# Half-size products for the down projection of two groups of SwiGLU tiles, with one gate/up unit placed in front of them

## The chip, the cores and the metric

The kernel runs on one core of a Trainium2 chip. The metric is the device time of one execution in microseconds. The time before is the median of three runs, 1265.05 us (1262.17 to 1267.66).

The core has five engines with a queue of instructions each, worked in order: TensorE (PE; its weight loads are listed as PEld), VectorE (DVE), ScalarE (ACT), GpSimd (POOL) and SyncE (SP). SP and POOL issue the transfers from memory here. An engine waits for another one by a semaphore, and everything behind the waiting instruction in its queue waits too.

## The reference

Two layers of an encoder on 512 tokens of width 1024. Each layer has a block of two attention-like halves (retention and differential attention) and a SwiGLU block. The change touches the SwiGLU block alone:

```python
h = rms_norm(x, ffn_norm_g[l])
x = x + (jax.nn.silu(h @ w_gate[l]) * (h @ w_up[l])) @ w_down[l]
```

`D_FF` is 2816, which is 22 tiles of 128. Everything is float32.

## The kernel before

**Layout.** Activations lie transposed: a tile has 128 features on the partitions and the 512 tokens along the row. `x` is eight such tiles, and the SwiGLU activation is 22. Products keep float32 accuracy by a split into two parts: `hi` is a rounded copy made by ACT (a CAST), `lo = src - hi` is made by DVE, and a product is three matmuls, hi·hi, hi·lo and lo·hi. So each weight and each activation that enters a product costs a cast on ACT and a subtraction on DVE of its size. The weights are the stationary side, so each matmul has a weight load of its own.

**The groups.** The SwiGLU block runs over the tiles in four groups, `FFN = [(0, 4), (4, 12), (12, 18), (18, FT)]` (L34). For each group, gate and up are computed tile by tile, and then the down projection of that group is added to the eight tiles of `x` (the loop over `m`; L205 to L207 are its matmuls, three for each tile of the group, 512 columns each; L634 is the addition to `x`).

**The plain group.** Group (0, 4) uses `gate_up`, with whole products of 512 columns. Beside it, DVE and ACT prepare with `combine` (L714 to L738) the sums of quarter blocks of h that the later groups need.

**The units.** For all later tiles, `seven` (from L754) computes gate and up of one tile, as a 2x2 block product, by seven half-size products in place of eight (the scheme of Strassen and Winograd): each product is 4 x 3 matmuls of 256 columns (L775), so 84 matmuls for a unit. The weight has four blocks of 512 columns. Three of the seven left sides are blocks as they are, and four are sums: `s31` holds two sums, made by transfers (a broadcast copy by SP, L756, and on top of it an accumulating transfer by POOL, L759); `a` gets its second half from DVE (the sum at L760); `s4` comes from DVE (L763). Then `split_in` splits three buffers of 1024 columns (ACT L740, DVE L741) and `split` splits `s4` (L223, L224). The products' sums go from three PSUM banks through ACT (L780, L783, L786) and DVE (L787, L789, L793, L795, L796), with a Silu on ACT (L106), and the result is split (L223, L224) for the down products.

**What sets the order.** A scheduler fixes the order of each engine's queue at build time, from data dependencies, free buffers and its own durations. By hand, units are interleaved: a unit's splits and first product stand ahead of the last product of the unit before. There are three buffers for the `hi` and three for the `lo` of weights (`NHL`), so a unit's three splits reuse those of the unit before as its products finish; weights land in three `raw` and three `ah` buffers (`four`), which is two units' worth. From the second unit on, the sum at L760 is kept behind the last split of the unit before (`last_split`, "unit by unit"); the first unit of each layer has no such tie.

Of the kernel before, what the change touches and what calls it, by code (L numbers as in the profile page):

```python
# [9 lines left out]
F32R = mybir.dt.float32r  # L10
AF = mybir.ActivationFunctionType
ALU = mybir.AluOpType

P = 128
# [19 lines left out]
FFN = [(0, 4), (4, 12), (12, 18), (18, FT)]  # L34
# [20 lines left out]
def encoder_kernel(ctx: ExitStack, tc: tile.TileContext, xT, wfirst, wsingle, wvv, wout, wgu, wdn, prm, lam, cst, outT):  # L55
# [15 lines left out]
    def big(s, dt=F32, tag="w", bufs=NW):  # L71
        return tpool.tile([P, T], dt, tag=tag, name=nm(s), bufs=bufs)
# [19 lines left out]
    def f32(ap):  # L92
        return ap.bitcast(F32)
# [84 lines left out]
    def parts():  # L178
        return tuple(wpool.tile([P, 1024], F32R, tag=t, name=nm(t), bufs=NHL) for t in ("hi", "lo"))
# [30 lines left out]
    def cut(pair, *idx):  # L210
        return tuple(t[idx] for t in pair)
# [9 lines left out]
    def split(src, tag, bufs):  # L221
        hi, lo = pair() if tag == "h" else [big(n, F32R, tag, bufs) for n in ("hi", "lo")]
        nc.scalar.copy(hi, src)  # L223
        nc.vector.tensor_tensor(lo, src, f32(hi), op=ALU.subtract)  # L224
        return hi, lo

# [83 lines left out]
    def layer(l, n1, h, x_src, first_raw):  # L310
# [395 lines left out]
        comb = []  # L706
# [8 lines left out]
        def combine(i):  # L715
# [14 lines left out]
            tb = split(tb, *(("mix", NMIX) if i else ("qk", NQK)))  # L730
            comb.append(
# [6 lines left out]
        def split_in(raw):  # L738
            hi, lo = parts()
            nc.scalar.copy(hi, raw)  # L740
            last_split[0] = nc.vector.tensor_tensor(lo, raw, f32(hi), op=ALU.subtract).ins.name  # L741
            return [(hi[:, i * T : (i + 1) * T], lo[:, i * T : (i + 1) * T]) for i in range(2)]
# [6 lines left out]
        fours, last_split = [0], [None]  # L749

        def seven(ff, act, tag, bufs):

            src = wgu[l, ff].rearrange("p (i n) -> p i n", n=T)
            s31, a, b, s4 = four(), four(), four(), big("s4")  # L754
            sums = s31.rearrange("p (i n) -> p i n", n=T)
            nc.sync.dma_start(sums, src[:, 1:2].broadcast_to([P, 2, T]))  # L756
            nc.sync.dma_start(a[:, :T], src[:, 0])
            nc.sync.dma_start(b, wgu[l, ff][:, 1024:])
            nc.gpsimd.dma_start(sums, src[:, 0::3], accum_op=ALU.add)  # L759
            i = nc.vector.tensor_tensor(a[:, T:], a[:, :T], s31[:, T:], op=ALU.add)  # L760
            if last_split[0]:
                tc.add_manual_dep(i.ins, last_split[0], order, reason="unit by unit")
            nc.vector.tensor_tensor(s4, b[:, :T], a[:, T:], op=ALU.add)  # L763
            g1, s2 = split_in(a)
            s3, s1 = split_in(s31)
            g2, u2 = split_in(b)
            s4 = split(s4, *(("w", NW) if ff >= FFN[-1][0] else ("mix", NMIX)))

            pa, pb, pc = (bank() for bank in (acc_bank, sc_bank, out_bank))

            def product(ps, w, r, start):
                for k in range(4):
                    L, R = cut(w, slice(None), slice(k * P, (k + 1) * P)), comb[k][r]
                    for i, (x1, x2) in enumerate(((0, 0), (0, 1), (1, 0))):
                        nc.tensor.matmul(ps[:, :C], L[x1], R[x2], start=start and k + i == 0, stop=k == 3 and i == 2, skip_group_check=True)  # L775
# [18 lines left out]
            func(g, g, AF.Silu)  # L794
            nc.vector.scalar_tensor_tensor(u[:, H1], pa[:, :C], -1.0, g[:, H1], op0=ALU.mult, op1=ALU.mult)  # L795
            nc.vector.tensor_tensor(u[:, H2], u[:, H2], g[:, H2], op=ALU.mult)  # L796
            act.append(split(u, tag, bufs))

        for a0, a1 in FFN:
            act, last = [], a1 == FT  # L800
            if a1 <= PLAIN:
                for ff in range(a0, a1):
                    act.append(gate_up(ff, *(("mix", NMIX) if ff < 2 else ("rn", 4))))
                    if ff:
                        combine(ff - 1)
            else:
                units = []
                for ff in range(a0, a1):
                    tag = ("h", 8) if not last else ("mix", NMIX) if ff < a0 + 2 else ("rn", 4)
                    units.append(seven(ff, act, *tag))  # L810
                next(units[0])
                for i, unit in enumerate(units):
                    next(unit)
                    if i + 1 < len(units):
                        next(units[i + 1])
                    next(unit, None)
            n = (a1 - a0) * P
            for m in range(KT):

                both = 2 * n <= 1024  # L820
                if not both or m % 2 == 0:
                    new = new_chunk(n * (1 + both), 1)
                    for i in range(1 + both):
                        nc.sync.dma_start(new[0][:, i * n : (i + 1) * n], wdn[l, m + i][:, a0 * P : a1 * P])
                    ww = split_chunk(*new)
                w = cut(ww, slice(None), slice(m % 2 * n, (m % 2 + 1) * n)) if both else ww
                if last and l + 1 == DEPTH and m == KT - 1:

                    for t, queue in ((H1, nc.sync), (H2, nc.scalar)):
                        ps = any_bank()  # L830
                        for i, a in enumerate(act):
                            mm3(ps[:, :C], cut(w, slice(None), slice(i * P, (i + 1) * P)), cut(a, slice(None), t), i == 0, i == a1 - a0 - 1)
                        nc.vector.tensor_tensor(x[m][:, t], x[m][:, t], ps[:, :C], op=ALU.add)
                        queue.dma_start(outT[m][:, t], x[m][:, t])
                    continue
                ps = any_bank()
                for i, a in enumerate(act):
                    mm3(ps, cut(w, slice(None), slice(i * P, (i + 1) * P)), a, i == 0, i == a1 - a0 - 1)
                if last and l + 1 < DEPTH:
                    residual(m, x[m], ps, n3, h3, PRM_AG + 8 * (l + 1))  # L840
                    nc.sync.dma_start(xscr[m], x[m])
                else:
                    residual(m, x[m], ps, None, None, None)
                    if a1 <= PLAIN and m == 1:
                        combine(PLAIN - 1)
                    if last:
                        nc.sync.dma_start(outT[m], x[m])
# [30 lines left out]
def _layout(inputs):  # L878
# [30 lines left out]
    a["wdn"] = w.transpose(0, 3, 2, 1, 4).reshape(DEPTH, KT, P, FT * P)  # L909
# [41 lines left out]
```

## Time and profile before

| | |
|---|---|
| median of three runs | 1265.05 us |
| the profiled execution's own time | 1264.07 us |
| its span, first to last instruction | 1262.3 us |
| its mean granted TensorE clock | 0.999 |
| matmul records | 7516 |
| first read of the plain group's gate and up sums (L690), layer by layer | 302.0 us and 926.6 us |
| last addition of a down projection to `x` (L634), last layer | 1256.6 us |

The profile is one execution. An engine's busy time is a union over the span; a busy PE need not be a PE at its peak, since matmuls overlap. In a timeline row, the number in brackets is the time the engine stood idle before the row, and what ended it. `raw`, `s` (the `ah` buffers), `hi`, `lo` are weights; `b`, `bh`, `bl`, `ta`, `tb` are the sums of h; `acc`, `sc`, `o` are PSUM banks. The names of a row in a queue's order carry a number, so that equal names can be told apart.

### The profile page before, as it was taken

The page shows a single profiled execution, that of the slowest core. Times are in us where ns is not written, and L with a number is a line of the kernel's source. Part 1 is how long each engine was busy: PE and PEld are TensorE (multiplying, and loading weights), DVE is VectorE, ACT ScalarE, POOL GpSimd, SP SyncE. Part 2 cuts the span into 40 slices and gives each one's busy share as a digit, 9 for nine tenths or more (in the row PEclk, how much of TensorE's full clock was granted, in tenths as well). Part 3 has the DMA queues.
Part 4 walks back from the last instruction along what each step waited for, and adds up shares of the span by engine and source line. Part 5 has one row for each costly group of instructions (what it writes and reads, how often), then busy time and mean ns, then how long its engine had stood idle before and what let it go on. Part 6 is the DMA issues. An engine that isn't in the chain of part 4 may idle for free.

```text
span 1262.3 us, 19138 instructions
## 1 busy us (share of the span) xinstructions
PE 1247.4 (99%) x7516; PEld 1100.3 (87%) x7516; DVE 915.8 (73%) x1514; ACT 674.1 (53%) x1106; POOL 61.4 (5%) x78
## 2 busy tenths in 40 slices
PE   9999999999899999999999999999999999999998
PEld 7878988778799989989888889987887999899897
DVE  6899768867877546747568997697778775576574
ACT  6778746555445425525448785565553553254251
POOL 1000000000011001000000000000000110000000
PEclk9999999999999999999999999999999999999999
DMA  7222223243277537646342122142333774476452
GB/s 264 84 68 67 68 67 125 68 116 101 71 176 174 166 102 166 163 114 151 110 156 84 51 84 67 51 150 77 99 101 84 174 182 129 119 180 152 122 140 84
DMA packets 58842, 148.48 MB, mean 118 GB/s; under 512 B 5632, under 2 KB 5888, under 8 KB 58624
## 3 DMA queue, kind: packets, MB, share of 16 engines
q1 hardware_dynamic: 48528, 127.95, 32.8%
q0 software_dynamic: 9792, 18.88, 9.4%
q8 instruction: 59, 0.97, 0.3%
q10 hardware_dynamic: 432, 0.44, 0.1%
q14 instruction: 31, 0.25, 0.1%
HBM read 143.05 MB, written 4.19 MB: 117 GB/s over the span
## 4 chain that ended last, share of the span: by engine, by line
PE 94%; DVE 3%; DMA 1%; ACT 1%; issue 0%; ACTq 0%
PE acc L775 16%; PE acc L205 11%; PE acc L207 11%; PE acc L206 11%; PE o L775 8%; PE o L205 4%; PE o L207 4%; PE sc L775 4%; PE o L206 4%; PE sc L207 4%; PE sc L205 4%; PE sc L206 3%; PE sc L400 2%; PE o L501 2%; PE sc L485 1%; DMA raw<-in_wgu 1%
## 5 line engine op out<-in xcount | busy, mean ns | idle before, releaser
L194 ACT CAST hi<-raw 128x1024 fp32r<-128x1024 f32 (+2 forms) x139 | 138.2, 1002 | 185.8 <-issue 49.2
L198 DVE TENSOR_TENSOR lo<-raw,hi 128x1024 fp32r<-128x1024 f32 (+2 forms) x140 | 162.1, 1162 | 58.8 <-ACT hi L194 58.4
L205 PE MATMUL acc<-h,hi 128*128 128x512 f32 x406 | 160.1, 396 | 0.6 <-ACT hi L194 0.6
L206 PE MATMUL acc<-h,hi 128*128 128x512 f32 x406 | 159.4, 393 | 0.0
L207 PE MATMUL acc<-h,lo 128*128 128x512 f32 x406 | 159.4, 393 | 0.0
L775 PE MATMUL acc<-hi,hi 128*128 128x256 f32 x432 | 123.2, 285 | 0.0
L775 PE MATMUL acc<-hi,lo 128*128 128x256 f32 x432 | 122.3, 283 | 0.0
L775 PE MATMUL acc<-lo,hi 128*128 128x256 f32 x432 | 122.3, 283 | 0.0
L740 ACT CAST hi<-raw 128x1024 fp32r<-128x1024 f32 x54 | 56.7, 1050 | 72.3 <-PE acc L775 42.2
L741 DVE TENSOR_TENSOR lo<-raw,hi 128x1024 fp32r<-128x1024 f32 x54 | 66.2, 1225 | 38.1 <-ACT hi L740 38.1
L740 ACT CAST hi<-s 128x1024 fp32r<-128x1024 f32 x54 | 56.6, 1048 | 67.3 <-issue 25.6
L205 PEld LDWEIGHTS acc<-h,hi 128*128 128x128 f32 x406 | 76.5, 189 | 17.6 <-ACT hi L194 1.9
L207 PEld LDWEIGHTS acc<-h,lo 128*128 128x128 f32 x406 | 76.6, 189 | 16.1 <-DVE lo L198 0.2
L206 PEld LDWEIGHTS acc<-h,hi 128*128 128x128 f32 x406 | 76.6, 189 | 15.2
L741 DVE TENSOR_TENSOR lo<-s,hi 128x1024 fp32r<-128x1024 f32 x54 | 66.2, 1226 | 25.4 <-ACT hi L740 25.4
L775 PEld LDWEIGHTS acc<-lo,hi 128*128 128x128 f32 x432 | 82.9, 192 | 0.2
L775 PEld LDWEIGHTS acc<-hi,hi 128*128 128x128 f32 x432 | 82.7, 192 | 0.2
L775 PEld LDWEIGHTS acc<-hi,lo 128*128 128x128 f32 x432 | 82.8, 192 | 0.0
L106 ACT ACTIVATE g<-g 128x512 f32<-128x512 f32 x44 | 27.8, 632 | 52.7 <-DVE g L793 47.8
L106 ACT ACTIVATE sc<-sc,mx 128x512 f32<-128x512 f32 x64 | 46.0, 720 | 18.4 <-DVE mx L404 17.9
L205 PE MATMUL sc<-h,hi 128*128 128x512 f32 x142 | 55.5, 394 | 0.0
L206 PE MATMUL sc<-h,hi 128*128 128x512 f32 x142 | 55.4, 390 | 0.0
(235 smaller groups left out, 3500.4 us busy)
## 6 DMA issues: line engine op xcount, KB each, us to landing
raw<-in_wgu SPq DMA_DIRECT2D x52, 512.0 KB, 4.2
s<-in_wgu SPq DMA_DIRECT2D x36, 512.0 KB, 4.7
raw<-in_wsingle SPq DMA_DIRECT2D x32, 512.0 KB, 3.6
s<-in_wgu POOLq DMA_DIRECT2D x18, 512.0 KB, 6.4
raw<-in_wgu POOLq DMA_DIRECT2D x18, 512.0 KB, 7.3
raw<-in_wvv SPq DMA_DIRECT2D x16, 512.0 KB, 3.6
raw<-in_wout SPq DMA_DIRECT2D x16, 512.0 KB, 3.6
raw<-in_wdn SPq DMA_DIRECT2D x32, 256.0 KB, 2.9
```

Of the source, the lines that this page charges most:

```text
L106: i = nc.scalar.activation(out, src, f, **kw).ins
L194: c = nc.scalar.copy(hi[:, s], raw[:, s])
L198: nc.vector.tensor_tensor(lo[:, s], raw[:, s], f32(hi[:, s]), op=ALU.subtract)
L205: first = nc.tensor.matmul(out, L[0], R[0], start=start, stop=False)
L206: nc.tensor.matmul(out, L[0], R[1], start=False, stop=False)
L207: nc.tensor.matmul(out, L[1], R[0], start=False, stop=stop)
L400: nc.tensor.matmul(ps, q[m][:, t], k[m][part], start=part == 0, stop=part == 1)
L485: nc.tensor.matmul(out, ks[hh][part][:, sb], qs[hh][:, tb], start=part == 0, stop=part == 1)
L501: i = nc.tensor.matmul(o[b, c * C : (c + 1) * C], v[pr // 2][2 * c + j][:, (pr % 2) * P + hh * HD : (pr % 2) * P + (hh + 1) * HD], s[c][:, ...
L740: nc.scalar.copy(hi, raw)
L741: last_split[0] = nc.vector.tensor_tensor(lo, raw, f32(hi), op=ALU.subtract).ins.name
L775: nc.tensor.matmul(ps[:, :C], L[x1], R[x2], start=start and k + i == 0, stop=k == 3 and i == 2, skip_group_check=True)
```

## The change

The groups become (0, 4), (4, 10), (10, 16), (16, 22). The down projection of the two middle groups, six tiles each, is computed by seven half-size products as well: the six activation tiles are the two row halves (three pairs of tiles), the two token halves are the columns, and `x` tiles m and m + 4 are the two output halves. `seven` is generalised: it takes its weight, a block width `n` (512 for gate/up, 384 for down), the right sides and a function `finish`. A down unit is 7 products of 3 x 3 matmuls of 256 columns, 63 in all, and there are four for each group; its weights come from a new array `wds`, laid out on the host in blocks of 384 columns.

Since the right sides are now sums of pairs of activation tiles, the first three units of a group end with `first_parts` (b11 and t1), the last three with `second_parts` (b2, t2, t3 and t4). `down(m)` adds a unit's result to `x[m]` and `x[m + 4]`. The list of units of a layer is one sequence: six gate/up units, then one gate/up unit of the next group, four down units, and the other five gate/up units, and the same again. The down projection of groups (0, 4) and (16, 22) stays plain. The first unit's sum is tied behind the last split of `combine`. In the last plain down projection of layer 0, the parts of h for the next layer (`next_part`) of tiles 4 to 7 stand behind all eight additions.

```diff
-FFN = [(0, 4), (4, 12), (12, 18), (18, FT)]
+FFN = [(0, 4), (4, 10), (10, 16), (16, FT)]
...
+            last_split[0] = splits[0]
...
-            if last_split[0]:
-                tc.add_manual_dep(i.ins, last_split[0], order, reason="unit by unit")
+            tc.add_manual_dep(i.ins, last_split[0], order, reason="unit by unit")
...
-            s4 = split(s4, *(("w", NW) if ff >= FFN[-1][0] else ("mix", NMIX)))
+            s4 = cut(split_to(s4, [big("s4", F32R, "mix", NMIX)[:, :n] for _ in range(2)]), slice(None))
...
-                for k in range(4):
-                    L, R = cut(w, slice(None), slice(k * P, (k + 1) * P)), comb[k][r]
+                for k in range(n // P):
+                    L, R = cut(w, slice(None), slice(k * P, (k + 1) * P)), right[k][r]
...
+            def first_parts(u, spread):
+                t = big("b11", F32R, *(("rn", 4) if spread else ("w", NW)))
+                t14 = pair()
+                b11 = split_to(u[:, H1], (t[:, H1], t[:, H2]))
+                nc.vector.tensor_tensor(u[:, H1], u[:, H1], u[:, H2], op=ALU.subtract)
+                t1 = split_to(u[:, H1], cut(t14, slice(None), H1))
+                act.append(dict(u=u, t14=t14, b11=b11, t1=t1))
+
+            def second_parts(u, o, spread):
+                v = o["u"]
+                b2 = split_to(u, [big("b2", F32R, "mix", NMIX) for _ in range(2)] if spread else pair())
+                nc.vector.scalar_tensor_tensor(v[:, H1], v[:, H1], -1.0, u[:, H2], op0=ALU.mult, op1=ALU.subtract)
+                nc.vector.tensor_tensor(v[:, H2], u[:, H2], v[:, H2], op=ALU.subtract)
+                t23 = split_to(v, pair())
+                nc.vector.scalar_tensor_tensor(u[:, H1], v[:, H1], -1.0, u[:, H1], op0=ALU.mult, op1=ALU.subtract)
+                t4 = split_to(u[:, H1], cut(o["t14"], slice(None), H2))
...
+        def down(m):
+            def finish(g, u, pa):
+                nc.vector.tensor_tensor(x[m], x[m], g, op=ALU.add)
+                nc.vector.tensor_tensor(x[m + 4][:, H2], x[m + 4][:, H2], u[:, H2], op=ALU.add)
+                nc.vector.tensor_tensor(x[m + 4][:, H1], x[m + 4][:, H1], pa, op=ALU.subtract)
...
+                ends = [activation(act, j, half, i > 0) for j in range(2 * half)]
+                downs.append([seven(wds[l, i, m], half * P, act, down(m)) for m in range(4)])
...
+        units = ups[0]
+        for d, u in zip(downs, ups[1:]):
+            units = units + u[:1] + d + u[1:]
```

**The first unit's sum, on DVE.** This is VectorE's queue at the end of the plain group of the first layer, before; L760 is the first unit's sum, the rows around it are the last `combine` and the split of the last plain activation (`lo_3334`).

```order
L719 SCALAR_TENSOR_TENSOR b_3401<-x_2615,prm_sb,rstd_2983 128x512
L719 SCALAR_TENSOR_TENSOR b_3402<-x_2770,prm_sb,rstd_2983 128x512
L712 TENSOR_TENSOR bl_3352<-b_3338,bh_3351 128x256
L728 TENSOR_TENSOR b_3355<-b_3338,b_3355 128x256
L760 TENSOR_TENSOR s_3536<-s_3536,raw_3535 128x512
L722 SCALAR_TENSOR_TENSOR ta_3341<-ta_3341,b_3338 128x256
L224 TENSOR_TENSOR lo_3334<-u_3330,hi_3333 128x512
L721 TENSOR_TENSOR ta_3405<-b_3401 128x256
L712 TENSOR_TENSOR bl_3412<-b_3401,bh_3411 128x256
L723 TENSOR_TENSOR tb_3406<-b_3402,b_3401 128x256
L712 TENSOR_TENSOR bl_3416<-b_3402,bh_3415 128x256
```

And this is the place in the queue after; L772 is the same sum, L636 adds the plain down products to `x`.

```order
L724 SCALAR_TENSOR_TENSOR ta_3405<-ta_3405,b_3402 128x256
L224 TENSOR_TENSOR lo_3363<-tb_3342,hi_3362 128x512
L726 SCALAR_TENSOR_TENSOR tb_3406<-ta_3405,b_3402 128x256
L730 TENSOR_TENSOR b_3419<-b_3402,b_3419 128x256
L224 TENSOR_TENSOR lo_3423<-ta_3405,hi_3422 128x512
L636 TENSOR_TENSOR x_2457<-x_2457,acc_3373 128x512
L224 TENSOR_TENSOR lo_3427<-tb_3406,hi_3426 128x512
L772 TENSOR_TENSOR s_3536<-s_3536,raw_3535 128x512
L636 TENSOR_TENSOR x_2513<-x_2513,sc_3387 128x512
L636 TENSOR_TENSOR x_2565<-x_2565,o_3437 128x512
L636 TENSOR_TENSOR x_2615<-x_2615,acc_3451 128x512
```

The sum has moved by fifteen rows, behind all that was left of `combine` (its last two splits are `lo_3423` and `lo_3427`) and the first addition to `x`.

**A unit's rows on DVE.** One cycle of a gate/up unit before, from one sum (L760) to the next, in the group (4, 12) of the first layer:

```order
L760 TENSOR_TENSOR raw_3898<-raw_3898,s_3897 128x512
L793 TENSOR_TENSOR g_3672<-o_3671,g_3672 128x256
L795 SCALAR_TENSOR_TENSOR u_3673<-acc_3669,g_3672 128x256
L796 TENSOR_TENSOR u_3673<-u_3673,g_3672 128x256
L741 TENSOR_TENSOR lo_3908<-raw_3898,hi_3907 128x1024
L789 TENSOR_TENSOR g_3799<-sc_3797,g_3799 128x256
L224 TENSOR_TENSOR h_3830<-u_3673,h_3830 128x512
L763 TENSOR_TENSOR s_3900<-s_3899,raw_3898 128x512
L741 TENSOR_TENSOR lo_3912<-s_3897,hi_3911 128x1024
L787 TENSOR_TENSOR u_3800<-u_3800,o_3798 128x256
L224 TENSOR_TENSOR lo_3920<-s_3900,hi_3919 128x512
L741 TENSOR_TENSOR lo_3916<-s_3899,hi_3915 128x1024
```

One cycle of a down unit after, in the first group; L750 are the weight splits, L744 the split of `s4`, L861 to L863 the additions to `x`:

```order
L772 TENSOR_TENSOR raw_4656<-raw_4656,s_4655 128x384
L804 TENSOR_TENSOR g_4474<-o_4473,g_4474 128x256
L750 TENSOR_TENSOR lo_4666<-raw_4656,hi_4665 128x768
L861 TENSOR_TENSOR x_2457<-x_2457,g_4474 128x512
L744 TENSOR_TENSOR s_4575<-s_4555,s_4574 128x384
L774 TENSOR_TENSOR s_4658<-s_4657,raw_4656 128x384
L800 TENSOR_TENSOR g_4581<-sc_4579,g_4581 128x256
L750 TENSOR_TENSOR lo_4670<-s_4655,hi_4669 128x768
L798 TENSOR_TENSOR u_4582<-u_4582,o_4580 128x256
L863 TENSOR_TENSOR x_2715<-x_2715,acc_4578 128x256
L862 TENSOR_TENSOR x_2715<-x_2715,u_4582 128x256
L750 TENSOR_TENSOR lo_4674<-s_4657,hi_4673 128x768
```

The result's four rows (L793, L795, L796 and the split L224) have become one (L804) and three additions to `x`; the operands are narrower.

**Where the first down unit enters, on PE.** TensorE's queue at the seam of the first middle group, after: `acc_4335` and `o_4337` belong to the gate/up unit of the next group that stands in front, `acc_4471` and `o_4473` to the first down unit, whose right sides (`b_3968`, `h_3705` and others) are parts of the group's activations.

```order
L786 MATMUL acc_4335<-lo_3427,hi_4327 128x256
L786 MATMUL acc_4335<-hi_3426,lo_4328 128x256
L786 MATMUL acc_4471<-b_3968,hi_4455 128x256 x2
L786 MATMUL acc_4471<-b_3968,lo_4456 128x256
L786 MATMUL o_4473<-h_3705,lo_4460 128x256
L786 MATMUL o_4473<-h_3837,hi_4459 128x256 x2
L786 MATMUL o_4473<-h_3837,lo_4460 128x256
L786 MATMUL o_4473<-h_3969,hi_4459 128x256 x2
L786 MATMUL o_4473<-h_3969,lo_4460 128x256
L786 MATMUL o_4337<-b_3153,s_4331 128x256 x2
```

Before, the group ended with whole down products at this kind of place; `sc_4432` is the last gate/up unit's bank, and `o_4557` a plain down product:

```order
L775 MATMUL acc_4431<-lo_3427,hi_4419 128x256
L775 MATMUL acc_4431<-hi_3426,lo_4420 128x256
L775 MATMUL sc_4432<-bl_3416,hi_4423 128x256
L775 MATMUL sc_4432<-bh_3415,lo_4424 128x256
L205 MATMUL o_4557<-h_3703,hi_4553 128x512
L206 MATMUL o_4557<-h_3703,hi_4553 128x512
L207 MATMUL o_4557<-h_3703,lo_4554 128x512
L205 MATMUL o_4557<-h_3830,hi_4553 128x512
```

So the whole products behind a group's last unit have given way to products that are interleaved with the next group's first unit.

More of the change, by code (lines that the diff above doesn't have):

```diff
@@ L223, in split @@
         nc.scalar.copy(hi, src)
-        nc.vector.tensor_tensor(lo, src, f32(hi), op=ALU.subtract)
+        splits[0] = nc.vector.tensor_tensor(lo, src, f32(hi), op=ALU.subtract).ins.name
         return hi, lo
+    splits = [None]
     def rsqrt(out, src, scale):
@@ L793, in seven @@
             nc.vector.tensor_tensor(g[:, H2], pc[:, :C], g[:, H2], op=ALU.add)
[L794 to L805, printed above, removed]
-            else:
[L807 to L841, printed above, removed]
-                else:
[L843 to L847, printed above, removed]
@@ new lines, in layer @@
+        ups, downs, later = [], [], []
+        for i, (a0, a1) in enumerate(FFN[1:]):
+            act, half = [], (a1 - a0) // 2
+            if a1 < FT:
+                ends = [activation(act, j, half, i > 0) for j in range(2 * half)]
+                downs.append([seven(wds[l, i, m], half * P, act, down(m)) for m in range(4)])
+            else:
+                ends = [plain(act, j) for j in range(2 * half)]
+            ups.append([seven(wgu[l, a0 + j], T, comb, end) for j, end in enumerate(ends)])
@@ L848, in layer @@
+        for m in late:
+            next_part(m)
         return n3, h3
```

135 lines of the change are left out of this document (114 added, 21 removed).

## The prediction

> **What bounds the kernel now.** I read the page's busy times first, then the chain of waits, then the table of 25 us windows over the SwiGLU block, to see where the bound holds and where it breaks.
>
> ```profile
> PE 1247.4 (99%) x7516; PEld 1100.3 (87%) x7516; DVE 915.8 (73%) x1514; ACT 674.1 (53%) x1106; POOL 61.4 (5%) x78
> PE 94%; DVE 3%; DMA 1%; ACT 1%; issue 0%; ACTq 0%
> ```
>
> TensorE is busy 99% of the span and makes 94% of the chain that ended last. So the time is the number of matmuls times their pitch, plus the few places where PE stands. In the windows (columns: length; busy time of PE, PEld, DVE, ACT and POOL with instruction counts; granted clock; DMA share; GB/s):
>
> ```profile
> 300.00:325.00 25.00, 25.00 (x112) 20.72 (x111) 24.07 (x42) 13.87 (x23) 0.00 (x0) 1.00 0.35 101
> 325.00:350.00 25.00, 21.77 (x94) 17.00 (x94) 20.96 (x38) 8.86 (x16) 1.21 (x1) 1.00 0.27 65
> 375.00:400.00 25.00, 25.00 (x208) 24.86 (x207) 19.85 (x31) 14.79 (x25) 2.57 (x3) 1.00 0.78 181
> 450.00:475.00 25.00, 25.00 (x112) 20.72 (x111) 10.31 (x13) 4.85 (x6) 1.20 (x1) 1.00 0.52 138
> 950.00:975.00 25.00, 21.86 (x88) 17.00 (x87) 21.33 (x38) 8.50 (x15) 1.20 (x1) 0.93 0.29 66
> ```
>
> 375 to 400 is a stretch of seven-product units, 450 to 475 one of plain down products: PE is full in both, and DVE has 5.15 us of 25 free in the first and 14.7 us in the second. The change moves work from the second kind into the first. The two windows where PE is not full, 325 to 350 and 950 to 975, are the ends of the plain groups, where the first unit's sum stands.
>
> **Change 1: the matmuls.** The price of a matmul is its pitch, from start to start in a full stretch (the duration in a row overlaps the next).
>
> ```profile
> 385.10 0.28 PE L775 MATMUL acc<-hi,hi 128*128 128x256 f32 x1
> ...
> 389.66 0.28 PE L775 MATMUL acc<-hi,lo 128*128 128x256 f32 x1
> ...
> 957.82 0.39 PE L205 MATMUL o<-hi,hi 128*128 128x512 f32 x1
> ...
> 964.39 0.39 PE L207 MATMUL acc<-hi,lo 128*128 128x512 f32 x1
> ```
>
> Between the first two lie 38 steps in 4.56 us, 0.120 us each; between the other two 29 steps in 6.57 us, 0.2266 us each. Before, groups of 4, 8, 6 and 4 tiles have plain down products; after, only 4 and the last 6 have. Each middle group gets four down units of 7 x 3 x 3 = 63 half-size matmuls: 2 layers x 2 groups x 4 x 63 = 1008, and plain products cut in two give 12 more, 1020 by the two queues. Whole-size matmuls go from 2980 to 2398, 582 fewer. So 582 x 0.2266 = 131.9 us go, 1020 x 0.120 = 122.4 us come: **-9.5 us**. That the product saves one in eight shows here as 7%, because 256 columns cost 0.53 of 512. The term vanishes at a half-size pitch of 131.9 / 1020 = 0.129 us.
>
> The Trainium skill, page "TensorE: Matmul & The Clock Gate", section "Back-to-back issue gap", gives about 81 ns at 128 columns and 131 ns at 512. By an estimate on a straight line that is some 98 ns at 256, three quarters of a whole one, and the exchange would lose 24 us. The rows here, 120 and 226.6 ns, disagree with it, and they decide.
>
> **Change 2: the first unit's sum.** It waits for the unit's last transfer, and on DVE it stands ahead of splits and additions that PE needs. Layer 0:
>
> ```profile
> 335.30 0.69 DVE L760 TENSOR_TENSOR s<-s,raw 128x512 f32<-128x512 f32 x1 [4.04 <-DMA raw<-in_wgu]
> ...
> 337.30 0.39 PE L206 MATMUL acc<-lo,hi 128*128 128x512 f32 x1
> ...
> 342.16 0.47 PE L205 MATMUL acc<-hi,hi 128*128 128x512 f32 x1 [1.98 <-DVE x L634]
> 343.27 0.50 PE L205 MATMUL sc<-hi,hi 128*128 128x512 f32 x1 [0.41 <-DVE x L634]
> ...
> 345.61 0.50 PE L207 MATMUL acc<-hi,lo 128*128 128x512 f32 x1 [0.63 <-DVE lo L198]
> ```
>
> DVE stands 4.04 us for a transfer, and soon after PE stands for additions to `x` (which free its banks) and for a `lo`. From 337.30 to 345.61 PE issues 16 whole and 4 half matmuls; at full pitch the last row would come at 337.30 + 16 x 0.2266 + 4 x 0.120 = 341.40. So 4.21 us are lost. Layer 1:
>
> ```profile
> 959.48 0.69 DVE L760 TENSOR_TENSOR s<-s,raw 128x512 f32<-128x512 f32 x1 [3.63 <-DMA raw<-in_wgu]
> ...
> 966.34 0.47 PE L205 MATMUL sc<-hi,hi 128*128 128x512 f32 x1 [1.56 <-DVE x L634]
> 967.45 0.50 PE L205 MATMUL o<-hi,hi 128*128 128x512 f32 x1 [0.41 <-DVE x L634]
> 969.78 0.80 PE L207 MATMUL sc<-hi,lo 128*128 128x512 f32 x1 [1.17 <-DVE lo L198]
> ...
> 975.71 0.39 PE L207 MATMUL o<-hi,lo 128*128 128x512 f32 x1
> ...
> 970.00:975.00 5.00, 5.00 (x16) 3.99 (x17) 4.96 (x7) 0.00 (x0) 0.00 (x0) 0.71 0.31 102
> ```
>
> From 964.39 to 975.71, 24 whole and 2 half matmuls would need 5.68 us and take 11.32: 5.64 us lost, some of it because the granted clock falls to 0.71 behind the waits. Both places together, 9.85 us, are the upper bound of this change; zero is the lower one. The sum's transfers keep their places in SP's and POOL's queues, so only DVE's order moves.
>
> What is late next? The tied sum stands behind the rest of `combine`, one `x` addition more than before, and the weight split of the last down tile stays behind the additions. Placing the new DVE queue of layer 0 by hand with pitches of back-to-back rows:
>
> ```profile
> 384.97 1.23 DVE L741 TENSOR_TENSOR lo<-s,hi 128x1024 fp32r<-128x1024 f32 x1
> 386.11 0.42 DVE L795 SCALAR_TENSOR_TENSOR u<-acc,g 128x256 f32<-128x256 f32 x1
> 386.44 0.42 DVE L796 TENSOR_TENSOR u<-u,g 128x256 f32<-128x256 f32 x1
> ...
> 389.55 0.68 DVE L224 TENSOR_TENSOR h<-u,h 128x512 fp32r<-128x512 f32 x1
> 390.15 0.69 DVE L224 TENSOR_TENSOR lo<-s,hi 128x512 fp32r<-128x512 f32 x1
> ...
> 550.25 1.82 DVE L198 TENSOR_TENSOR lo<-raw,hi 128x768 fp32r<-128x768 f32 x2
> ```
>
> These give 1.14 us for 1024 columns, 0.33 for 256, 0.60 for 512, and for 768 (1.82 - 0.09 overlap) / 2 = 0.87. Where the sum stood idle at 331.26, nine operations of 256 and four of 512 columns (5.4 us) can now run, to 336.6. The first addition to `x` follows its bank at 338.0, the last `combine` split ends at 339.2, the sum (its data landed at 335.3) at 339.8, three additions by 341.6, and the split of 768 columns at 342.7. The row of 345.61 then comes at about 343.1: 2.5 us of 4.2 are gained, and what is left waits for that split. In layer 1 the same placing leaves about 1.6 of 5.64 us, without the clock's fall: 4.0 gained. **-6.5 us**, between 0 and -9.85.
>
> On the clock the Trainium skill, the same page, section "HAM clock gate", says that PE's clock is lowered by idle time, and that gaps above some 3 us should be avoided. Layer 1 agrees in part, 3.14 us of waits and then 0.71; layer 0 has 3.02 us and keeps 1.00, so I count the clock only in layer 1.
>
> **Change 3: sixteen more units.** A unit's seams are not free:
>
> ```profile
> 383.13 0.68 DVE L760 TENSOR_TENSOR s<-s,raw 128x512 f32<-128x512 f32 x1
> ...
> 393.20 0.69 DVE L760 TENSOR_TENSOR raw<-raw,s 128x512 f32<-128x512 f32 x1
> ...
> 403.45 0.69 DVE L760 TENSOR_TENSOR s<-s,raw 128x512 f32<-128x512 f32 x1
> ```
>
> Two periods take 20.32 us, where 168 matmuls at 0.120 take 20.16: 0.08 us a unit, so 16 x 0.08 = **+1.3 us**.
>
> **Change 4: what DVE, ACT and the queues get.** A gate/up unit now costs DVE one split and sum of 512 or 256 columns each: rows L760 to L741 of the order add to 3 x 1.14 + 3 x 0.60 + 0.60 + 5 x 0.33 = 7.47 us of a period of 10.16. A first-half unit has 3 x 0.33 in place of one 0.60: 7.86. A second-half unit adds two splits of 512, three operations of 256 and a split of 256 and drops one of 512: 7.47 - 0.60 + 1.20 + 4 x 0.33 = 9.39. A down unit has 3 x 0.87 + 0.60 + 3 x 0.47 + 5 x 0.33 = 6.27 us of 63 x 0.120 = 7.56 (0.47 for 384 columns lies between 0.33 and 0.60). All are below PE's period, so the matmuls hide them; 9.39 of 10.16 leaves little. The transfers:
>
> ```profile
> s<-in_wgu SPq DMA_DIRECT2D x36, 512.0 KB, 4.7
> s<-in_wgu POOLq DMA_DIRECT2D x18, 512.0 KB, 6.4
> ...
> raw<-in_wdn SPq DMA_DIRECT2D x16, 384.0 KB, 3.7
> ```
>
> A down unit needs its copy on SP and then the accumulating transfer on POOL, and the sum stands behind them on DVE, with the splits that PE needs behind it. At 512 columns this takes 4.7 + 6.4 = 11.1 us from the release of the buffer; the shape of 384 is in no row for it, and by 3.7 against 4.7 for loads it would take 8.7. The order leaves one and a half periods of 7.56, 11.3 us, less the casts ahead, about 10. So DVE waits 0 to 1.1 us a unit, and its free 7.56 - 6.27 = 1.29 us cover even that. The cover is gone where DVE also waits for a cast:
>
> ```profile
> DVE lo L741 <- ACT hi L740: 63.5, 84, 2.9
> ...
> 628.20 0.50 PE L205 MATMUL acc<-h,hi 128*128 128x512 f32 x1 [0.60 <-ACT hi L194]
> ```
>
> That is 63.5 / 84 = 0.76 us each, so PE could lose 1.1 + 0.76 - 1.29 = 0.57 us a unit, 9 us over 16. Between 0 and 9 I take **+1.5 us**, near the end to which the loads of 384 columns point, for this and the splits' waits together. `next_part` of four tiles moves behind the additions at the end of layer 0, where PE waits 0.60 us for a cast now (the second row); I count nothing: in TensorE's queue 48 whole products of the next layer on tiles 0 to 3, 10.9 us, stand ahead of the first one that reads tile 4. Without that cover it would cost the cast's wait and a split, some 1.4 us.
>
> **The sum.** The profiled execution took 1264.07 us, 0.98 below the median of the runs. 1264.07 - 9.5 - 6.5 + 1.3 + 1.5 = 1250.9, **1251 us**.
>
> **The rivals.**
>
> **A: DVE cannot keep up in the second-half units.** Today DVE idles 5.15 of 25 us, 2.1 a unit, waiting for casts and banks that it cannot have earlier. If that idle time stays, a cycle is 9.39 + 2.1 = 11.5 us against 10.16: 1.3 us for each of 3 units x 4 groups, 16 us at most, none if the buffers' lead (worked out in B) absorbs it; in the middle 1251 + 8 = 1259. For it: DVE's waits for casts, as in change 4. Against: DVE runs ahead of PE by up to a unit.
>
> **B: slower. The handoff from ACT in the new splits.** A second-half unit gets three more splits, whose input DVE makes, whose cast ACT makes, and on which DVE then waits 0.76 us as above: 2.3 more, a cycle of 13.8 us if nothing fills it. That is 3.6 us over PE's in 12 units, 44 us. Three split buffers hold three of seven products ahead, 4.35 us, once in each of four groups, 17 us. What is left is +26: 1277 us. The sign turns where the cycle passes 10.16 + (13 + 17) / 12 = 12.7 us, 13 being the forecast's gain and 17 the leads. Against it: in the queues other rows lie between such operations.
>
> **C: the first unit's wait only moves on**, so change 2 gives nothing: 1251 + 6.5 = 1257.5. For it: the transfer lands as late as before, and additions to `x` still follow.
>
> **D: all new costs are hidden**, and change 2 gives its bound: 1264.07 - 9.5 - 9.85 = 1244.7.
>
> **E: the half-size pitch in down units is above 0.129**, so change 1 gives nothing: 1260.4 or more. The products are the same kind as today's, so little speaks for it.
>
> **How the numbers follow.** The forecast's case (1247 to 1256) gets 0.60, A 0.15, B 0.06, C 0.10, D 0.06, E 0.03. The range 1245 to 1259 holds the forecast, D, C and half of A: 0.60 + 0.05 + 0.09 + 0.08 = 0.82. A measurement of this kernel can tell about 0.5%, which is 6.3 us of 1265.05: under 1258.7 counts as faster, over 1271.4 as slower. Faster: the forecast, C, D and half of A less the tails, 0.80; the rest of A, E and tails between, 0.13; B and A with a share of it, 0.07.
>
> **What would show it.** In the changed kernel's profile, PE's windows in the middle groups must stay at 25.00 with the clock at 1.00, and the pitch in down units at 0.120. At the end of the plain groups PE's idle times should fall from 3 us to under 1.5, the idle time before the first sum should be gone, and layer 1's clock should stay at 1.00. Late right sides show as PE idle behind a cast or a split (L223, L224 or the new parts), late buffers as a sum that waits for a POOL transfer in the down units. The prediction is wrong if these waits pass some 9 us in all, or if the plain groups' ends still lose over 5 us each.

## The result, and the profile after

The change makes the kernel slower: 1279.14 us (median of 4 runs, 1275.09 to 1285.12) against 1265.22 us before, a ratio of 1.0113 with a 95% interval of 1.0073 to 1.0153. The forecast was 1251 us and a range of 1245 to 1259. The profiled execution is the longest of the four, with an own time of 1285.12 us, 21.05 more than that of before.

The page of the changed kernel, busy times and chain:

```profile
PE 1246.0 (97%) x7954; PEld 1119.9 (87%) x7954; DVE 997.7 (78%) x1734; ACT 724.8 (56%) x1230; POOL 80.6 (6%) x94
...
PE 91%; DMA 3%; DVE 3%; ACT 1%; issue 1%; ACTq 0%
```

And its windows of 25 us (columns as in the prediction):

```profile
325.00:350.00 25.00, 24.13 (x124) 20.12 (x123) 22.42 (x40) 9.37 (x15) 1.21 (x1) 1.00 0.38 91
...
450.00:475.00 25.00, 22.02 (x161) 21.66 (x162) 19.56 (x32) 12.30 (x20) 3.61 (x3) 0.86 0.67 156
...
950.00:975.00 25.00, 25.00 (x112) 20.70 (x111) 23.43 (x47) 12.00 (x22) 1.21 (x1) 1.00 0.35 85
...
1175.00:1200.00 25.00, 18.56 (x136) 18.06 (x135) 14.31 (x25) 8.29 (x15) 3.11 (x3) 0.86 0.66 159
```

The two holes at the ends of the plain groups (325 to 350, 950 to 975) are nearly closed. New ones stand in the middle groups, with the clock down to a mean of 0.86, and the chain now has 3% of transfers. What PE and DVE waited for in the whole span (total, times, longest):

```profile
PE acc L786 <- ACT hi L749: 21.7, 8, 5.9
...
PE o L786 <- ACT hi L749: 2.6, 4, 0.9
...
DVE raw L772 <- DMA s<-in_wgu: 24.3, 4, 7.4
```

DVE waits four times for a transfer of gate/up weights, once in each middle group's seam: where the first gate/up unit follows four down units. The timelines of SP, POOL, DVE and PE at the first seam (L768 is the copy of the two sums, L771 the accumulating transfer, L772 the sum that DVE makes of them):

```profile
434.34 0.38 SPq L768 DMA_DIRECT2D s<-in_wgu  x1
...
440.64 1.20 POOL L771 DMA_DIRECT2D s<-in_wgu  x1 [8.98 <-DVE s L744]
440.88 0.33 SPq L769 DMA_DIRECT2D s<-in_wgu  x1
442.03 0.38 SPq L768 DMA_DIRECT2D raw<-in_wgu  x1
444.21 0.33 SPq L770 DMA_DIRECT2D raw<-in_wgu  x1
...
450.54 0.69 DVE L772 TENSOR_TENSOR raw<-raw,s 128x512 f32<-128x512 f32 x1 [6.36 <-DMA s<-in_wgu]
...
447.28 0.28 PE L786 MATMUL sc<-b,lo 128*128 128x256 f32 x1
452.41 0.58 PE L786 MATMUL acc<-bh,hi 128*128 128x256 f32 x1 [4.85 <-ACT hi L749]
...
453.77 0.58 PE L786 MATMUL o<-hi,hi 128*128 128x256 f32 x1 [0.57 <-ACT hi L749]
454.15 0.41 PE L786 MATMUL o<-lo,hi 128*128 128x256 f32 x1
...
456.28 0.41 PE L786 MATMUL acc<-bh,lo 128*128 128x256 f32 x1
...
458.37 0.28 PE L786 MATMUL acc<-hi,hi 128*128 128x256 f32 x1
```

The accumulating transfer lands 9.9 us after its issue, DVE's sum waits 6.36 us for it, the cast behind the sum comes late, and PE stands for 4.85 and 0.57 us. After that PE is slow: 454.15 to 456.28 are 10 steps of 0.213 us instead of 0.120. From 447.28 to 458.37 there are 24 steps, 2.88 us at full pitch, and they take 11.09: **8.2 us lost at one seam**. In the waits above, the four seams have 21.7 - 4 x 0.85 (the four other ones, below) + 2.6 = 20.9 us of idle time; counted like the first one, they lose 8.2, 8.2, 6.6 and 9.0 us, together about **32 us**, so some 11 us of it are slow steps.

Two smaller waits come once in each group, at the last second-half unit and at the second down unit (timeline of PE):

```profile
394.93 0.39 PE L786 MATMUL acc<-bh,lo 128*128 128x256 f32 x1 [0.64 <-DVE lo L750]
...
423.16 0.50 PE L786 MATMUL acc<-b,hi 128*128 128x256 f32 x2 [0.85 <-ACT hi L749]
```

From start to start these steps lose 0.80 and 1.01 us, 7.2 us in four groups. The sum, then: -9.5 (matmuls) - 7.0 (first sums, from 9.85 to 1.4 at each of two places by the same count) + 32 + 7.2 = +22.7, against 21.05 measured.

### The profile page after: what moved, and what is told of

It reads as the page before. It is cut to its first block, busy times and chain, and to the rows that moved or that the text cites. A ratio compares the mean times of both kernels' runs of the same rounds, so it can differ in the third digit from the quotient of the medians.

```text
span 1283.0 us, 20476 instructions
## 1 busy us (share of the span) xinstructions
PE 1246.0 (97%) x7954; PEld 1119.9 (87%) x7954; DVE 997.7 (78%) x1734; ACT 724.8 (56%) x1230; POOL 80.6 (6%) x94
## 4 chain that ended last, share of the span: by engine, by line
PE 91%; DMA 3%; DVE 3%; ACT 1%; issue 1%; ACTq 0%
PE acc L786 20%; PE o L786 10%; PE acc L205 10%; PE acc L207 10%; PE acc L206 10%; PE sc L786 5%; PE o L205 3%; PE o L207 3%; PE o L206 3%; DMA s<-in_wgu 3%; PE sc L205 3%; PE sc L207 3%; PE sc L206 3%; PE sc L402 2%; PE o L503 2%; PE sc L487 1%
## 5 line engine op out<-in xcount | busy, mean ns | idle before, releaser
L205 PE MATMUL acc<-h,hi 128*128 128x512 f32 (+1 forms) x344 | 134.7, 393 | 1.0 <-ACT h L216 1.0
L207 PE MATMUL acc<-h,lo 128*128 128x512 f32 (+1 forms) x344 | 134.5, 391 | 0.0
L206 PE MATMUL acc<-h,hi 128*128 128x512 f32 (+1 forms) x344 | 134.4, 391 | 0.0
L749 ACT CAST hi<-raw 128x1024 fp32r<-128x1024 f32 (+1 forms) x78 | 76.6, 982 | 94.3 <-DVE raw L772 36.3
L749 ACT CAST hi<-s 128x1024 fp32r<-128x1024 f32 (+1 forms) x78 | 76.6, 982 | 68.7 <-PE acc L786 26.7
L750 DVE TENSOR_TENSOR lo<-raw,hi 128x1024 fp32r<-128x1024 f32 (+1 forms) x78 | 88.9, 1139 | 23.4 <-ACT hi L749 22.9
L750 DVE TENSOR_TENSOR lo<-s,hi 128x1024 fp32r<-128x1024 f32 (+1 forms) x78 | 88.9, 1139 | 18.1 <-ACT hi L749 17.6
L786 PE MATMUL o<-b,s 128*128 128x256 f32 x480 | 66.0, 283 | 0.0
L786 PE MATMUL acc<-bh,hi 128*128 128x256 f32 x144 | 44.3, 308 | 19.4 <-ACT hi L749 18.3
L786 PEld LDWEIGHTS o<-b,s 128*128 128x128 f32 x480 | 61.4, 192 | 0.2
L786 PE MATMUL acc<-h,hi 128*128 128x256 f32 x288 | 57.0, 293 | 0.0
```

Of the source, the lines that this page charges most:

```text
L205: first = nc.tensor.matmul(out, L[0], R[0], start=start, stop=False)
L206: nc.tensor.matmul(out, L[0], R[1], start=False, stop=False)
L207: nc.tensor.matmul(out, L[1], R[0], start=False, stop=stop)
```

## The experiments

Every run was compared with the kernel before on the same chip (medians 1263.9 to 1264.7 us).

**The tie alone**, in the kernel before:

```diff
+            last_split[0] = splits[0]
...
-            if last_split[0]:
-                tc.add_manual_dep(i.ins, last_split[0], order, reason="unit by unit")
+            tc.add_manual_dep(i.ins, last_split[0], order, reason="unit by unit")
```

> The kernel before with one part of the change alone: the first unit's sum is tied behind the last split of combine; groups and down products stay as they were. Both theories of the loss at the seams leave this part alone. If the tie is worth what PE's lost time at the plain groups' ends shows in the changed kernel (4.2 and 5.6 us before, 1.4 and 1.4 after), the time falls by about 7 us, to 1258. If the stall merely moved to another place, it stays within 2 us of before.

Measured 1256.14 us against 1264.05, ratio 0.9944 (0.9929 to 0.9959): 7.9 us. The tie is worth what was read from PE's lost time.

**The changed kernel without the tie:**

```diff
-            tc.add_manual_dep(i.ins, last_split[0], order, reason="unit by unit")
+            if fours[0] > 3:
+                tc.add_manual_dep(i.ins, last_split[0], order, reason="unit by unit")
```

> The changed kernel with the tie of the first unit's sum taken out, everything else as it is. If the parts add up, the plain groups' ends lose 4 to 6 us each again and the time is 7 to 8 us above the changed kernel's 1279, at 1286 to 1287. Rival: the seams' stalls absorb it (the transfers behind get ahead while PE stands), and the time stays within 3 us of 1279.

Measured 1288.76 us, ratio 1.0178 (1.0158 to 1.0197), 9.6 us above the changed kernel. The parts add up: the loss belongs to the rest of the change, the down units and their groups, and by 1279.14 - 1256.14 this rest costs about 23 us where 9.5 were to be saved.

**The transfers behind the seam held back**, so that two of the three loads that run beside the accumulating transfer come later (the third, 256 KB, is not held):

```diff
+            if hold:
+                for t in (s31, b):
+                    m = nc.vector.memset(t[:, :1], 0.0)
+                    tc.add_manual_dep(m.ins, sum_of[0], order, reason="hold")
             nc.sync.dma_start(sums, blocks[:, 1:2].broadcast_to([P, 2, n]))
```

> The changed kernel, but at each seam (first gate/up unit after four down units) the copy and the pair of blocks of the unit behind it may start only after the seam unit's sum (a one-column memset on DVE behind that sum stands in front of them). Theory contention: the seam's accumulating transfer is slow (9.9 us from issue to sum) because those transfers run beside it; alone it takes about 6.5 us, PE's idle time at each seam falls from 3.4 to 5.9 us to 0 to 2.5 us, and the total falls by some 12 us. Theory buffer period: the transfers start too late because the buffer is released a fixed time ahead and down units are shorter; the accumulating transfer still lands 3 us or more late at each seam, and the unit behind now waits as well, so the total stays or grows.

Measured 1298.24 us, ratio 1.0277 (1.0262 to 1.0292). SP, POOL and DVE at the first seam and the unit behind it:

```profile
440.75 0.33 SPq L773 DMA_DIRECT2D s<-in_wgu  x1
...
440.84 1.20 POOL L775 DMA_DIRECT2D s<-in_wgu  x1 [9.32 <-DVE s L779]
...
447.14 0.69 DVE L776 TENSOR_TENSOR raw<-raw,s 128x512 f32<-128x512 f32 x1 [3.10 <-DMA s<-in_wgu]
...
462.48 0.69 DVE L776 TENSOR_TENSOR s<-s,raw 128x512 f32<-128x512 f32 x1 [5.56 <-DMA raw<-in_wgu]
```

The same transfer, issued at the same time, lands in 6.3 us instead of 9.9. So it was slowed by its neighbours, but even beside the one load that is left it is 3.10 us late, and the held unit is later still. Neither theory has it all: some 3 us of DVE's wait are contention with the two held loads, some 3 are there without them.

**A buffer of its own** for the seam unit's sum that DVE needs first (256 KB, a copy and an accumulating transfer to itself), so that it starts earlier; and then for both sums, with one working tile fewer (`NW` 11):

```diff
+            if seam:
+                s31 = [four()[:, :n], big("s", F32, "seam", 1)]
...
+                for t, k in ((s31[1], 3), (s31[0], 0)):
+                    nc.gpsimd.dma_start(t, blocks[:, k], accum_op=ALU.add)
```

> The changed kernel, but at each seam the one sum that DVE needs first has a 2 KB buffer of its own, so that its copy and accumulating transfer (256 KB each) need not wait for a buffer of an earlier unit; the other sum takes the usual buffer. Nothing else changes. Theory buffer period: PE's idle time at the seams (4.85, 4.17, 3.40, 5.87 us) falls to under 1 us each, the clock stays at 1.00 there, and the total falls by 20 to 28 us, to about 1253 to 1258. Theory contention: the DMA engines are full there and an early start only moves the bytes, 3 us or more of idle time stay at each seam, and the total falls by under 8 us.

> As the run with one sum's own buffer, but both sums of the seam unit have buffers of their own (4 KB), for which the pool of working tiles has 11 in place of 12 buffers in the whole kernel. Theory buffer period: the seams' idle time goes as there, and a cost of the smaller pool shows elsewhere, 0 to 10 us. Theory contention: 3 us or more stay at each seam.

One buffer: 1270.57 us (1262.84 to 1276.33, 10 runs), ratio 1.0056 (1.0037 to 1.0075). Both: 1259.53 us, ratio 0.9968 (0.9951 to 0.9985). The seam's sum in the run with one buffer, and what DVE waits for in its whole span:

```profile
443.77 0.68 DVE L795 TENSOR_TENSOR raw<-raw,s 128x512 f32<-128x512 f32 x1
...
DVE s L795 <- DMA raw<-in_wgu: 11.6, 4, 3.5
```

The sum comes at 443.77 with no wait, 6.8 us earlier than in the changed kernel, and PE's two waits at this seam are 0.34 and 0.45 us. So with this transfer early enough the stall is gone at this unit. That alone doesn't part a late start from contention: a transfer that starts a group ahead (POOL issues the next seam's at 458.13) meets neither, and it is half as large. And the time fell by only 8.6 us, since the unit behind now waits. The same kernel once more, because its times spread so widely:

> The kernel of the run with one sum's own buffer once more, for a second profile, since its times lie between 1262.8 and 1276.3 and its first profile is of the shortest. Theory buffer period: the seams are free again, and what differs is the unit behind the seam, whose sum then waits for its transfer (3.5 us at most in the first profile). Rival: the longer runs are longer everywhere, by a lower clock.

```profile
DVE s L795 <- DMA raw<-in_wgu: 19.1, 7, 3.6
```

This execution took 1268.71 us at a clock of 1.000. It is longer by waits for transfers (19.1 us in 7 places instead of 11.6 in 4), not by its clock. I read this as transfers with no lead to spare, where small differences in landing times show; that is one execution, and the longest of the ten, 1276.33 us, had a mean clock of 0.993.

**Down units in pairs**, with a gate/up unit between the pairs; first with two activation tiles of the next group exchanged (which changes the data and not the work), then with the tiles in order:

```diff
-            units = units + u[:1] + d + u[1:]
+            units = units + u[:1] + d[:2] + u[1:2] + d[2:] + u[2:]
```

> The changed kernel with the order of units in a middle group's seam altered: one gate/up unit, two down units, one gate/up unit, two down units, then the other gate/up units; nothing else. Theory buffer period: what counts is that two short down units stand ahead of a full-size gate/up unit; there are now eight such seams in place of four, each idle 3 to 5 us, and the time grows by 15 to 30 us over the changed kernel, to 1295 to 1310. Theory contention or a backlog of bytes that builds up over four down units: the load is spread, each seam's idle time falls to under half, and the time is no longer than the changed kernel's 1279.

> The kernel with two down units, a gate/up unit and two more down units, as before, but the activation tiles of the next group are kept in their order (in the earlier run two of them were exchanged, which changes data and not the work). Theory, a run of four short units uses up the lead of the transfers: the time is that of the earlier run, 1263, 16 us under the changed kernel, with PE's idle time at the first gate/up unit behind each pair under 0.6 us. Rival, the order of the tiles let work start earlier there: the time goes back above 1270.

Measured 1263.03 us and 1262.91 us, ratios 0.9997 (0.9981 to 1.0013) and 0.9989 (0.9969 to 1.0009). My theory said 1295 to 1310; it was wrong. With no added buffer, 16 us went. POOL and DVE at the first gate/up unit behind a pair:

```profile
420.55 1.20 POOL L771 DMA_DIRECT2D s<-in_wgu  x1 [9.55 <-DVE h L744]
...
428.49 0.68 DVE L772 TENSOR_TENSOR raw<-raw,s 128x512 f32<-128x512 f32 x1
```

Two short units ahead of a full one are not enough to stall it: the transfer is issued 7.9 us ahead of the sum and is in time. What counts is the run of four. In the changed kernel the last down unit's copy, POOL's issues and DVE's sums of the down units stand like this:

```profile
426.59 0.38 SPq L768 DMA_DIRECT2D raw<-in_wds  x1
...
402.66 1.20 POOL L771 DMA_DIRECT2D s<-in_wds  x1 [9.94 <-DVE g L804]
410.35 1.20 POOL L771 DMA_DIRECT2D raw<-in_wds  x1 [6.48 <-DMA raw<-in_wds]
...
419.77 1.20 POOL L771 DMA_DIRECT2D s<-in_wds  x1 [8.22 <-DVE s L772]
...
430.46 1.20 POOL L771 DMA_DIRECT2D raw<-in_wds  x1 [9.48 <-DMA raw<-in_wds]
...
410.35 0.55 DVE L772 TENSOR_TENSOR raw<-raw,s 128x384 f32<-128x384 f32 x1
...
419.22 0.55 DVE L772 TENSOR_TENSOR s<-s,raw 128x384 f32<-128x384 f32 x1
...
428.95 0.55 DVE L772 TENSOR_TENSOR raw<-raw,s 128x384 f32<-128x384 f32 x1
...
436.51 0.55 DVE L772 TENSOR_TENSOR s<-s,raw 128x384 f32<-128x384 f32 x1
```

From issue to sum these are 7.7, 8.9, 9.2 and 6.1 us. For the seam unit, whose sum is due at about 436.51 + 7.56 = 444.1, 3.5 us are left. The first three sums still stand 8.9 and 9.7 us apart, and the lead holds. Then the sums come every 7.56 us, the time in which PE uses up a down unit, while the issues come 9.4 to 10.7 us apart (410.35, 419.77, 430.46, 440.64): within two units the lead falls from 9.2 to 3.5 us, and the fifth issue, a full-size one, needs more than that. In the first kernel with pairs, by the same rows, the six units from the first down unit to the gate/up unit behind the second pair have leads of 7.9, 9.0, 7.9, 7.2, 7.4 and 6.4 us. (In the second of the two runs PE's waits behind the pairs reach 1.7 us, more than was expected.)

**Order around the second-half units**, on top of both buffers, in two attempts:

```diff
+                i = nc.vector.scalar_tensor_tensor(v[:, H1], v[:, H1], -1.0, u[:, H2], op0=ALU.mult, op1=ALU.subtract)
+                tc.add_manual_dep(i.ins, ahead, order, reason="behind the next unit's split")
...
+                        if r == "b11" and k + i == 0 and behind and last_mm[0]:
+                            tc.add_manual_dep(mm, last_mm[0], order, reason="behind u2")
```

> The run with both seam sums in buffers of their own, and two ties more: on DVE the first combination of a second-half unit (the subtraction that makes t2) stands behind the first weight split of the next unit, and on PE the second down unit's first product stands behind the sixth product of the first one. Theory: the two waits that every middle group still shows (0.64 us for a split, 0.85 us for a cast, 0.8 and 1.0 us of lost pitch) come from the order in which the scheduler put these rows, not from DVE's load; both go, 7.2 us in all, and the time falls from 1259.5 to about 1253. Rival, DVE cannot keep up in second-half units: the waits only move to the next split, and the time stays at 1259.

Measured 1266.51 us, ratio 1.0019 (1.0001 to 1.0037): the waits of 0.64 and 0.85 us stayed, and one of 1.12 came beside them. The tied split was that of the next unit, which had run anyway; the one that PE waits for belongs to the unit after. The second attempt issues the combinations one unit later and puts the parts of t2 and t3 ahead of the first down unit's second split:

```diff
-                second_parts(u, act[i], spread)
+                    pend.append(lambda: second_parts(u, act[i], spread, first_split[0]))
...
+                for i, d in zip((a, b), behind):
+                    tc.add_manual_dep(i.ins, d, order, reason="behind t2 and t3")
```

> The run with both seam sums in buffers of their own, with another order around the second-half units than the two ties tried: the combinations of a second-half unit stand behind the first weight split of the unit after the next (they are issued one unit later), and at the group's end the casts and splits of t2 and t3 stand ahead of the first down unit's second weight split. Theory, the order makes the two waits of 0.64 and 0.85 us: both fall below 0.2 us in all four groups, and the time falls by 4 to 7 us, from 1259.5 to about 1254. Rival, DVE's load in second-half units makes them: they move or grow, and the time does not fall by more than 2 us.

Measured 1257.46 us, ratio 0.9928 (0.9904 to 0.9952), 2.1 us under the run with both buffers. The first wait:

```profile
393.53 0.38 PE L820 MATMUL acc<-bh,lo 128*128 128x256 f32 x1 [0.30 <-DVE lo L753]
```

It fell from 0.64 to 0.30 us, and the one of 0.85 to at most 0.44; from start to start the steps now lose 3.2 us in four groups instead of 7.2. So the order makes somewhat more than half of these 7.2 us; whether the rest is DVE's load is not shown. The time gained less than expected: at a gate/up unit further on DVE's sum now waits 4.75 us for its transfer, and PE stands 4.2.

**All that helped, and one that didn't:**

> The parts that helped, together: the tie of the first unit's sum, down units in pairs with a gate/up unit between them, both sums in buffers of their own for the gate/up unit behind each pair, and the order of the second-half units from the run before. Theory, lead of the transfers: neither a pair nor the units behind it use up the lead, PE's idle time at the seams and behind them is under 0.6 us everywhere in the middle groups, and the time is 1250 to 1254, under all runs so far. Rival, the bytes themselves: over the whole stretch of seven-product units the transfers have no lead to spare, waits of 1 to 4 us come up at some gate/up unit in any order, and the time stays at 1256 to 1260.

> The run with the other order of the second-half units, but both sums have buffers of their own in two gate/up units behind each four down units instead of one. Theory, lead of the transfers: the stall of 4.2 us at the third gate/up unit (568 us in that run's profile) comes from lead that the four down units used up and that the second one still lacks; it falls under 1 us, the time falls by 2 to 5 us to 1253 to 1255. Rival, the bytes themselves: the stall comes up at a later unit, and the time stays at 1257 to 1260.

All together: 1254.50 us (1253.98 to 1255.08), ratio 0.9921 (0.9896 to 0.9945), the fastest of all, 9.5 us under before. But the tie alone gave 1256.14, ratio 0.9944: what the down units, with all that helped, add to it is 1.6 us by the medians and 2.9 by the ratios, and the two intervals overlap. So no run here shows the 9.5 us that change 1 saves in matmuls as time; where they went was not followed. DVE's one wait for a gate/up transfer:

```profile
DVE raw L802 <- DMA s<-in_wgu: 1.2, 1, 1.2
```

Against it, the kernel of the second attempt, with its four down units in a row, but with buffers of their own in two consecutive units: 1283.91 us, ratio 1.0150 (1.0120 to 1.0179).

```profile
DVE s L802 <- DMA s<-in_wgu: 15.1, 4, 3.9
```

Expected were 1253 to 1255. I had given both units the one pair of buffers, so that the second unit's copy starts only when the first has used it; it is late in all four groups. It is the same lesson once more: a buffer that is released one unit ahead is released too late.

## Why the prediction was wrong

**The step that failed** is change 4, on the transfers: "DVE waits 0 to 1.1 us a unit, and its free 7.56 - 6.27 = 1.29 us cover even that". For the down units themselves it held: DVE waits for none of their transfers, and the last one has 9.9 us from its copy (426.59) to its sum (436.51), the "about 10" of the prediction. But it priced each down unit for itself, with transfers of 384 columns and a fixed lead. Three things were left out. The lead is a stock that is carried from unit to unit: issues 9.4 to 10.7 us apart against a use every 7.56 draw it down. The unit that pays is the full-size gate/up unit behind them, which I did not price at all: it has 9.8 us from its copy (434.34) to the time when its sum is due, and by the prediction's own 11.1 us for 512 columns that is 1.3 too few. And the two transfers took 16.2 us in place of 11.1: 6.3 from the copy to POOL's issue, and 9.9 for the accumulating transfer beside the loads of the unit behind. The 6.4 us between 16.2 and 9.8 are DVE's wait. The term was +1.5 us, bounds 0 to 9; it measured about 32 at the seams and 7.2 at the small waits. Pairs take 16 us of this away and buffers of their own for both sums 20; both change how early the transfers can be issued.

**Change 1, matmuls: right**, and rival E with it wrong. The half-size pitch holds in the down units. In the changed kernel's timeline of PE, 36 matmuls lie between these two rows, 4.32 us, 0.120 each:

```profile
432.25 0.40 PE L786 MATMUL acc<-b,hi 128*128 128x256 f32 x2
...
436.57 0.88 PE L786 MATMUL o<-h,s 128*128 128x256 f32 x6
```

**Change 2, the first sum: right**, -6.5 forecast, -7.9 measured alone, which speaks against rival C. What is late next is what was named, an addition to `x` and the last split, at both ends 0.55 and 0.32 us (layer 0's rows):

```profile
340.05 0.36 PE L786 MATMUL acc<-bh,hi 128*128 128x256 f32 x1 [0.55 <-DVE x L636]
...
341.09 0.50 PE L207 MATMUL acc<-hi,lo 128*128 128x512 f32 x1 [0.32 <-DVE lo L198]
```

**Change 3, the seams between units:** +1.3 us; no run prices it by itself, and the sum of the result closes within 1.7 us without it.

**The other rivals.** A and B looked for the slower side in DVE's work and in casts. The mechanism was wrong: the second-half units' waits are there, but as two rows in each group, which the order makes in part, and they cost 7.2 us, under A's 16. The slower side came from the transfers. The sign turns where the seams cost more than changes 1 and 2 save beyond the small waits, 9.5 + 7.0 - 7.2 = 9.3 us, or 2.3 at each of the four.

**The clock.** What the prediction cites from the Trainium skill, "TensorE: Matmul & The Clock Gate", section "HAM clock gate", that idle time lowers PE's clock, is borne out here: behind each of the four stalls of 3.4 to 5.9 us the half-size matmuls took 0.213 us instead of 0.120. Its bound of some 3 us is not: one wait of 1.88 us was enough (last section). I left the clock out of the price of a wait in change 4. It is some 11 of the 32 us (2.8 at the first seam).

**What stays open:** how much of the 32 us is contention. At the first seam two neighbours took the transfer from 6.3 to 9.9 us, but holding them back only moved the loss. And which transfers differ between a short and a long execution of one kernel was not followed beyond the counts above.

## What to carry to other kernels

Work in units has a lead, the time from a transfer's issue to its use. When units become shorter, compare the period at which their transfers can be issued with the period at which they are used up; a run of short units spends the difference from a stock, and the first full-size unit behind them pays. Mixing short and long units brought 16 us here, and giving that one unit buffers that are free earlier, for all that it waits for, 20; both only won back what the short units had lost. Price a wait of the matrix engine with the slow matmuls behind it.

## What the runs showed of the hardware

An idle stretch of PE can cost half as much again in clock: behind 5.42 us of waits at the first seam, 2.8 us went to slow matmuls, most of them at 0.213 us instead of 0.120. How long an idle stretch must be for that was not steady. In the first kernel with pairs, a wait of 1.88 us had a mean clock of 0.89 in the 15 us around it and matmuls of 0.213 us behind it, and one of 1.81 us a clock of 1.00 (the two windows, in the columns as above):

```profile
474.00:489.00 15.00, 13.12 (x97) 12.92 (x96) 9.64 (x17) 7.37 (x13) 1.38 (x2) 0.89 0.71 179
1196.00:1211.00 15.00, 13.19 (x110) 12.91 (x109) 12.20 (x21) 8.94 (x14) 1.20 (x1) 1.00 0.44 116
```

An accumulating transfer of 512 KB that POOL issued took 9.9 us to land beside three loads of 1.3 MB, and 6.3 us with two of the three held back (both at the first seam).
